# RWKV's transfers around the forward substitution: issued by GpSimd instead of SyncE

## Chip, cores and metric

One core of one Trainium2 chip. The metric is the device time of one execution of the whole program in microseconds, the median of several runs. Engines are named as in the profile: PE = TensorE, DVE = VectorE, ACT = ScalarE, POOL = GpSimd, SP = SyncE. A DMA is issued by an engine's queue; here every DMA is issued by SP.

## What is computed

One layer (1024 tokens, width 1024) of a hybrid decoder trunk. The part around the change is the RWKV-7 group: four heads of 64, a state updated token by token.

```python
def step(S, inp):
    r_t, w_t, k_t, v_t, kk_t, a_t = inp
    sa = jnp.einsum('bhvk,bhk->bhv', S, -kk_t)
    S = S * w_t[:, :, None, :] + sa[..., None] * (kk_t * a_t)[:, :, None, :] + v_t[..., None] * k_t[:, :, None, :]
    return S, jnp.einsum('bhvk,bhk->bhv', S, r_t)
...
mix = jnp.concatenate([y_conv, y_nsa, y_rwkv], axis=-1)
x = x + mix @ w_out[i]
```

Beside it stand a convolution group (31 taps, LayerNorm) and a sparse-attention group; all three go through one output projection, then a gated MLP and a final norm follow.

## The kernel before

The kernel works in the stages projections (with RWKV and convolution beside them, to about 380 us), attention (from about 400 to 733 us, with RWKV beside it), output projection, MLP up and MLP down.

RWKV is done in chunks of 64 tokens. Two pairs of heads `j` and two halves of the sequence `h` give four units, 00, 01, 10 and 11. Each has four steps: `rwkv_prep` and `rwkv_mats` (S), `rwkv_solve` (V), `rwkv_chain` (C). They are written in the order S00 .. V00 S01 .. C00 V01 .. S10 C01 V10 S11 C10 V11 C11, all at high priority. Most of their PSUM results take turns in the two banks of the tag `rw`.

In S, the chunk matrices come out of PE and DVE masks them into `GA` (L497). The inverse of their triangular part is found in blocks of 32 x 32 by forward substitution: 31 steps, each one product (L528, `sx`) and one sum (L530, `sT`) on POOL. To bring 32 small systems into one partition layout the data passes through DRAM:

- L503: four stores `dn<-GA` (two after each of the two `GA`), each 256 pieces of 128 B;
- L506: four loads `sN<-dn`, each 32 rows of 4 KB; L528 of the first step waits for them;
- after the substitution DVE transposes the result (L532, `sTT`); L534: four stores `dt<-sT`, each 512 pieces of 32 B; L535: four stores `dtt<-sTT`, each 256 pieces of 128 B;
- in V, L543: one load `DF<-dt` and L546, L547: two loads of `dtt` into `sN`, each 512 pieces of 128 B; the first matmul (L550) waits for L543, the second (L556) for the other two.

That is 19 DMAs for a unit and 76 in all. An engine executes its list in order; a DMA that waits for data holds up what is listed behind it on the same engine. The order of each engine's list is made at build time by a scheduler with a timing model, by readiness and priority. POOL also runs the taps of the second half of the convolution channels (L279, `cacc`, fed by ACT's L278, `ctap`), the differences of the down-projection weights (L945 to L948) and two steps of each attention tile (L849, L857, `cmp`). DVE splits every weight into two parts (L121, `wlo`), which PE needs for each projection (L229), and runs the taps of the first half of the channels (L272).

Of the kernel before, what the change touches and what calls it, by code (L numbers as in the profile page):

```python
# [19 lines left out]
class K:  # L20
# [460 lines left out]
    def rwkv_mats(self, u):  # L481
        nc = self.nc
        v, s, pe = nc.vector, nc.scalar, nc.tensor
        dn = self.dram.tile([32, 32, 32], F32, name=f"dn{u.j}{u.h}")
        u.dt = self.dram.tile([16, 32, 4, 8], F32, name=f"dt{u.j}{u.h}")
        u.dtt = self.dram.tile([32, 8, 4, 32], F32, name=f"dtt{u.j}{u.h}")
        u.GA, u.GR = [], []
        for x, G in enumerate((u.GA, u.GR)):
            pts = [self.bank(u.tp) for _ in range(2)]
            for c in range(8):  # L490
                for hp in range(2):
                    r = slice(hp * 64, hp * 64 + 64)
                    pe.matmul(pts[hp][:, c * 64:c * 64 + 64], u.BK[c // 4][r, c % 4].rearrange("p a t -> p (a t)"),  # L493
                              u.r[r, c, :] if x else u.VAc[c // 4][r, c % 4, 1, :], start=True, stop=True)
            for hp in range(2):
                Gm = self.rb([P, 8, 64], name="GR" if x else "GA")
                v.tensor_tensor(Gm, pts[hp].rearrange("p (a b) -> p a b", b=64),  # L497
                                self.gmask[:, x * 64:x * 64 + 64].unsqueeze(1).to_broadcast([P, 8, 64]), op=ALU.mult)
                G.append(Gm)
                if not x:  # L500
                    for blk in range(2):
                        p0 = blk * 16 + hp * 8
                        nc.sync.dma_start(dn[p0:p0 + 8].rearrange("p s t -> s p t"), Gm[64 + blk * 32:96 + blk * 32, :, blk * 32:blk * 32 + 32])  # L503
        N = self.sN.rearrange("p (a b) -> p a b", b=32)
        for g in range(4):
            nc.sync.dma_start(N[g * 32:g * 32 + 32], dn)  # L506
        u.VA, u.KB = [], []
        for q in range(2):
            VA = self.rb([P, 4, P], name="VA")
            KB = self.rb([P, 4, P], name="KB")  # L510
            BK = u.BK[q].rearrange("p c a t -> p c (a t)")
            v.tensor_tensor(BK, BK, u.PC[:, q * 4:q * 4 + 4].unsqueeze(2).to_broadcast([P, 4, P]), op=ALU.mult)
            for dst in (VA, KB):
                pt = self.bank(u.tp)
                for c in range(4):
                    x = u.VAc[q][:, c].rearrange("p a t -> p (a t)") if dst is VA else BK[:, c, :]
                    pe.transpose(pt[:, c * P:c * P + P], x, self.idn)
                s.activation(dst.rearrange("p c x -> p (c x)"), pt, AF.Copy)
            u.VA.append(VA)
            u.KB.append(KB)  # L520

        Tm = self.sT
        nc.gpsimd.tensor_copy(Tm, self.sI)
        for q in range(31):
            n, w = 31 - q, q // 4 + 1
            x = self.sx[:, 0:n * w].rearrange("p (a b) -> p a b", b=w)
            v_ = getattr(nc, self.B["sub"])
            v_.tensor_tensor(x, N[:, q, q + 1:32].unsqueeze(2).to_broadcast([P, n, w]),  # L528
                            Tm[:, q, 0:w].unsqueeze(1).to_broadcast([P, n, w]), op=ALU.mult)
            v_.tensor_tensor(Tm[:, q + 1:32, 0:w], Tm[:, q + 1:32, 0:w], x, op=ALU.add)  # L530
        sTT = self.sTT.rearrange("p a b -> p (a b)").rearrange("p (a b) -> p a b", b=32)
        v.tensor_copy(sTT, Tm.rearrange("p a b -> p b a"))  # L532
        for g in range(4):
            nc.sync.dma_start(u.dt[:, :, g, :], Tm[g * 32:g * 32 + 16])  # L534
            nc.sync.dma_start(u.dtt[:, :, g, :], sTT[g * 32:g * 32 + 32])  # L535

    def rwkv_solve(self, u):
        nc = self.nc
        s, pe = nc.scalar, nc.tensor

        TT = self.sN.rearrange("p (a b) -> p a b", b=64)
        DF = self.DF
        nc.sync.dma_start(DF[64:96], u.dt.rearrange("p s g c -> s p (g c)"))  # L543
        nc.gpsimd.memset(TT[96:128, :, 0:32], 0.0)
        dtt = u.dtt.rearrange("p c g t -> (c g) p t")
        nc.sync.dma_start(TT[64:96, :, 0:32], dtt[:, 0:16])  # L546
        nc.sync.dma_start(TT[96:128, :, 32:64], dtt[:, 16:32])  # L547
        pt = self.bank("rw")
        for p in range(16):
            pe.matmul(pt[96:128, p * 32:p * 32 + 32], u.GA[p // 8][64:96, p % 8, 32:64], DF[64:96, p, :], start=True, stop=True,  # L550
                      tile_position=(64, 96))

        s.activation(DF[96:128].rearrange("p a (c g) -> p a c g", g=4), pt[96:128].rearrange("p (a g c) -> p a c g", g=4, c=8), AF.Copy)
        pt = self.bank("rw")
        for p in range(16):
            pe.matmul(pt[64:96, p * 32:p * 32 + 32], DF[96:128, p, :], TT[96:128, p, 32:64], start=True, stop=True,  # L556
                      tile_position=(96, 64))
        s.activation(TT[64:96, :, 32:64], pt[64:96].rearrange("p (a b) -> p a b", b=32), AF.Copy)

        pa = self.bank("rw")  # L560
        for c in range(8):
            for hp in range(2):
                pe.matmul(pa[hp * 64:hp * 64 + 64, c * 64:c * 64 + 64], u.VA[c // 4][64:128, c % 4, hp * 64:hp * 64 + 64],
                          TT[64:128, hp * 8 + c, :], start=True, stop=True)
        s.activation(u.AT.rearrange("p a b -> p (a b)"), pa, AF.Copy)
        for hp in range(2):
            x = slice(hp * 64, hp * 64 + 64)
            W = self.rt(name="W")
            pt = self.bank("rw")
            for c in range(8):  # L570
                pe.matmul(pt[64:128, c * 64:c * 64 + 64], u.GA[hp][0:64, c, :], u.VA[c // 4][0:64, c % 4, x], start=True, stop=True)
            s.activation(W[64:128], pt[64:128], AF.Copy)
            pt = self.bank("rw")
            for c in range(8):
                pe.matmul(pt[64:128, c * 64:c * 64 + 64], TT[64:128, hp * 8 + c, :], W[64:128, c * 64:c * 64 + 64], start=True, stop=True)
            for q in range(2):
                s.activation(u.VA[q][64:128, :, x], pt[64:128, q * 256:q * 256 + 256].rearrange("p (c x) -> p c x", x=64), AF.Copy)
# [823 lines left out]
```

## Time and profile before

| | |
|---|---|
| median of 3 runs | 1515.36 us (1514.93 to 1518.39) |
| the profiled execution | 1516.71 us, its span 1515.0 us |
| PE busy | 1418.2 us (94% of the span) |
| DVE busy | 1001.0 us (66%) |
| ACT busy | 684.0 us (45%) |
| POOL busy | 500.2 us (33%) |
| DMA packets issued | 206564, all on SP's queue |

PE is busy nearly throughout, so a change shows in the end only where it makes or removes a time in which PE has nothing to do. A row of the timeline reads: start in us, duration, engine, line, operation, output<-inputs, shape, count; in brackets the idle time before it and what ended that.

### The profile page before, as it was taken

To read this page: it belongs to the slowest core of one execution; us is meant where nothing else is said; L and a number is where in the kernel's file an instruction comes from. 1 tells how busy PE (TensorE), PEld (TensorE's weight loads), DVE (VectorE), ACT (ScalarE), POOL (GpSimd) and SP (SyncE) were. 2 spreads that over 40 slices of the span, in tenths; PEclk is the share of its full clock that TensorE was granted. 3 is DMA by queue.
4 is the path that set the end of the run, shared out by engine and by line. 5 is a ranking of instruction groups with operands and counts; after the bars stand their busy time and mean duration, and the time that the engine had idled before them with its cause. 6 is when DMAs were issued, how large, how long until landed. Compare 5 with 4: busy or idle time off the path is not lost.

```text
span 1515.0 us, 22973 instructions
## 1 busy us (share of the span) xinstructions
PE 1418.2 (94%) x8025; PEld 1128.7 (75%) x8025; DVE 1001.0 (66%) x2171; ACT 684.0 (45%) x1361; POOL 500.2 (33%) x607
## 2 busy tenths in 40 slices
PE   6999688999798999999599899999999999999997
PEld 5887566777666777767478677888888788888886
DVE  5346696454488587777446776775876876666675
ACT  5432255534155665776333353333333443445463
POOL 1003887910487204100000133453453443113310
PEclk9999887999699999999899999999999999999999
DMA  6133223434888301310742113332332333986633
GB/s 184 36 105 80 46 77 95 146 89 119 246 259 270 101 21 41 81 43 16 226 121 84 57 56 98 105 112 84 104 119 91 104 104 111 383 295 213 207 91 111
DMA packets 206680, 186.71 MB, mean 123 GB/s; under 512 B 56355, under 2 KB 145764, under 8 KB 206564
## 3 DMA queue, kind: packets, MB, share of 16 engines
q1 hardware_dynamic: 206564, 185.24, 39.5%
q8 instruction: 63, 1.03, 0.3%
q14 instruction: 53, 0.43, 0.1%
HBM read 126.99 MB, written 58.20 MB: 122 GB/s over the span
## 4 chain that ended last, share of the span: by engine, by line
PE 78%; DVE 10%; DMA 4%; POOL 2%; issue 2%; ACT 2%; SPq 1%; DVEq 0%; ACTq 0%; POOLq 0%
PE mm L229 13%; PE gb L229 12%; PE rw L229 10%; PE ga L229 8%; PE gc L229 8%; PE tr L229 5%; PE tr L918 4%; PE av L926 4%; PE mm L893 2%; PE mm L894 2%; POOL sx L528 1%; PE rw L493 1%; POOL sT L530 1%; DVE pp L897 1%; DVE pp L911 1%
## 5 line engine op out<-in xcount | busy, mean ns | idle before, releaser
L229 PE MATMUL mm<-hT,whi 128*128 128x512 f32 x608 | 201.6, 413 | 0.0
L229 PE MATMUL mm<-hT,wlo 128*128 128x512 f32 x304 | 126.1, 416 | 18.8 <-DVE wlo L121 18.8
L229 PEld LDWEIGHTS mm<-hT,whi 128*128 128x128 f32 x608 | 118.3, 197 | 28.5 <-issue 1.4
L921 ACT ACTIVATE pT<-tr 128x512 f32<-128x512 f32 (+1 forms) x152 | 79.8, 536 | 62.1 <-PE tr L918 59.0
L926 PE MATMUL av<-pT,V 128*64 128x128 f32 x1056 | 96.4, 289 | 1.3 <-ACT pT L921 1.1
L279 POOL TENSOR_TENSOR cacc<-cacc,ctap 128x512 f32<-128x512 f32 x60 | 91.6, 1550 | 15.0 <-ACT ctap L278 14.9
L229 PE MATMUL rw<-woh,mix 128*128 128x512 f32 x240 | 79.4, 406 | 17.0 <-ACT mix L120 17.0
L918 PE MATMUL tr<-idn,pp 128*128 128x128 f32 x528 | 91.6, 292 | 0.5 <-DVE pp L911 0.3
L121 DVE TENSOR_TENSOR sp<-rb,sp 128x512 fp32r<-128x512 f32 x66 | 57.1, 865 | 50.4 <-ACT sp L120 50.3
L1072 POOL TENSOR_TENSOR S<-wraw,wr 128x512 f32<-128x512 f32 x22 | 28.5, 1295 | 181.0 <-DVE or L107 79.2
L229 PEld LDWEIGHTS mm<-hT,wlo 128*128 128x128 f32 x304 | 59.9, 197 | 37.0 <-DVE wlo L121 20.1
L893 PE MATMUL mm<-KH,QS 128*128 128x512 f32 (+2 forms) x192 | 77.3, 407 | 10.0 <-DVE mx L897 7.7
L229 PE MATMUL rw<-sp,sp 128*128 128x512 f32 x330 | 86.1, 389 | 0.0
L229 PE MATMUL tr<-sp,sp 128*128 128x512 f32 x330 | 85.9, 389 | 0.0
L926 PEld LDWEIGHTS av<-pT,V 128*64 128x64 f32 x1056 | 59.9, 138 | 27.3 <-issue 13.0
L528 POOL TENSOR_TENSOR sx<-sN,sT 128x60 f32<-128x60 f32 (+24 forms) x124 | 47.4, 382 | 97.4 <-DMA sN<-dn 90.5
L918 PEld LDWEIGHTS tr<-idn,pp 128*128 128x128 f32 x528 | 56.5, 142 | 30.0 <-issue 27.9
L120 ACT ACTIVATE sp<-rb 128x512 fp32r<-128x512 f32 x66 | 41.6, 630 | 74.0 <-PE tr L229 37.5
L121 DVE TENSOR_TENSOR sp<-b,sp 128x512 fp32r<-128x512 f32 x88 | 68.8, 789 | 5.3 <-ACT sp L120 5.1
L229 PEld LDWEIGHTS rw<-sp,sp 128*128 128x128 f32 x330 | 62.0, 188 | 12.8
L229 PEld LDWEIGHTS tr<-sp,sp 128*128 128x128 f32 x330 | 62.0, 188 | 12.8
L904 ACT ACTIVATE pp<-pp,nm 128x640 f32<-128x640 f32 (+3 forms) x64 | 57.6, 904 | 23.7 <-DVE nm L902 22.1
(457 smaller groups left out, 3721.0 us busy)
## 6 DMA issues: line engine op xcount, KB each, us to landing
wraw<-in_ffn_w_up_dram SPq DMA_DIRECT2D x44, 256.0 KB
wr<-in_ffn_w_gate_dram SPq DMA_DIRECT2D x44, 256.0 KB
pdS<-prod SPq DMA_DIRECT2D x44, 256.0 KB
b<-pdS SPq DMA_DIRECT2D x44, 256.0 KB
rb<-tdT SPq DMA_DIRECT2D x44, 256.0 KB
pdA<-prod SPq DMA_DIRECT2D x33, 256.0 KB
b<-pdA SPq DMA_DIRECT2D x33, 256.0 KB
wraw<-in_w_in_dram SPq DMA_DIRECT2D x30, 256.0 KB
```

The source lines that it names most:

```text
L120: self.nc.scalar.activation(hi, src, AF.Copy)
L121: getattr(self.nc, eng).tensor_tensor(lo, src, hi.bitcast(F32), op=ALU.subtract)
L229: mm = lambda l, r, **k: self.nc.tensor.matmul(out, l, r, skip_group_check=more, **k)
L279: nc.gpsimd.tensor_tensor(t[:, o:o + 512], t[:, o:o + 512], z, op=ALU.add)
L528: v_.tensor_tensor(x, N[:, q, q + 1:32].unsqueeze(2).to_broadcast([P, n, w]), Tm[:, q, 0:w].unsqueeze(1).to_broadcast([P, n, w]), op=ALU.mult)
L893: pe.matmul(pts[g][:, 0:n], QS[:, r, g, :], KH[g][hf][:, ks], start=True, stop=False)
L894: pe.matmul(pts[g][:, 0:n], QS[:, r, g, :], KL[g][hf][:, ks], start=False, stop=True)
L904: s.activation(Ps[g], Ps[g], AF.Exp, bias=nm[:, g:g + 1], scale=-1.0, accum_out=sm[:, g:g + 1])
L918: pe.transpose(pt[:, o:o + P], Ps[g][:, kt * P:kt * P + P], self.idn)
L921: s.activation(pT[:, 0:n], pt[:, 0:n], AF.Copy)
L926: pe.matmul(av[g * 64:g * 64 + 64, r * P:r * P + P], self.V[kk // 2][:, kk % 2, vo + g * 64:vo + g * 64 + 64], pT[:, o:o + P], start=first ...
L1072: gp.tensor_tensor(t, x, y, op=op)
```

## The change

All 76 of these DMAs are issued by GpSimd's queue instead of SP's. Nothing else is edited: sizes, layouts, buffers and the order in which the program is written stay. The lists of all engines are made anew by the scheduler.

```diff
@@ rwkv_mats
-                        nc.sync.dma_start(dn[p0:p0 + 8].rearrange("p s t -> s p t"), Gm[64 + blk * 32:96 + blk * 32, :, blk * 32:blk * 32 + 32])
+                        nc.gpsimd.dma_start(dn[p0:p0 + 8].rearrange("p s t -> s p t"), Gm[64 + blk * 32:96 + blk * 32, :, blk * 32:blk * 32 + 32])
         for g in range(4):
-            nc.sync.dma_start(N[g * 32:g * 32 + 32], dn)
+            nc.gpsimd.dma_start(N[g * 32:g * 32 + 32], dn)
...
         for g in range(4):
-            nc.sync.dma_start(u.dt[:, :, g, :], Tm[g * 32:g * 32 + 16])
-            nc.sync.dma_start(u.dtt[:, :, g, :], sTT[g * 32:g * 32 + 32])
+            nc.gpsimd.dma_start(u.dt[:, :, g, :], Tm[g * 32:g * 32 + 16])
+            nc.gpsimd.dma_start(u.dtt[:, :, g, :], sTT[g * 32:g * 32 + 32])
@@ rwkv_solve
-        nc.sync.dma_start(DF[64:96], u.dt.rearrange("p s g c -> s p (g c)"))
+        nc.gpsimd.dma_start(DF[64:96], u.dt.rearrange("p s g c -> s p (g c)"))
         nc.gpsimd.memset(TT[96:128, :, 0:32], 0.0)
         dtt = u.dtt.rearrange("p c g t -> (c g) p t")
-        nc.sync.dma_start(TT[64:96, :, 0:32], dtt[:, 0:16])
-        nc.sync.dma_start(TT[96:128, :, 32:64], dtt[:, 16:32])
+        nc.gpsimd.dma_start(TT[64:96, :, 0:32], dtt[:, 0:16])
+        nc.gpsimd.dma_start(TT[96:128, :, 32:64], dtt[:, 16:32])
```

## Rows read from the trace of the kernel before

**Rows 1.** Windows: span, busy us of each engine, PE clock, DMA share, GB/s

```profile
150.00:180.00 30.00, 17.99 (x79) 13.33 (x78) 16.44 (x23) 5.08 (x9) 22.27 (x52) 0.83 0.10 17
560.00:640.00 80.00, 79.86 (x701) 61.60 (x699) 61.98 (x242) 48.08 (x122) 21.20 (x66) 1.00 0.23 56
...
sum 1515.00, PE 1418.16 PEld 1128.75 DVE 1001.02 ACT 683.98 POOL 500.18; mean PE 88.63 PEld 70.55 DVE 62.56 ACT 42.75 POOL 31.26
```

**Rows 2.** Instructions of tiles dn, dt, dtt: ns of one issue, min/median/max

```profile
L503 SPq DMA_DIRECT2D dn<-GA x16: 302/442/568, 125.0 to 579.1; - x16
L506 SPq DMA_DIRECT2D sN<-dn x16: 302/414/647, 132.1 to 582.4; - x16
...
L534 SPq DMA_DIRECT2D dt<-sT x16: 561/608/1107, 173.5 to 617.1; - x16
...
L535 SPq DMA_DIRECT2D dtt<-sTT x16: 549/613/1012, 178.2 to 617.7; - x16
```

**Rows 3.** Timeline of unit 00, DVE, SP, POOL and PE, 129 to 180 us

```profile
129.17 0.69 DVE L497 TENSOR_TENSOR GA<-pm,gmask 128x512 f32<-128x512 f32 x1 [2.40 <-PE pm L493]
...
132.12 1.71 SPq L506 DMA_DIRECT2D sN<-dn  x4
...
136.26 0.39 POOL L528 TENSOR_TENSOR sx<-sN,sT 128x31 f32<-128x31 f32 x1 [37.59 <-DMA sN<-dn]
...
160.27 0.34 POOL L530 TENSOR_TENSOR sT<-sT,sx 128x76 f32<-128x76 f32 x1
...
173.51 0.69 DVE L532 COPY sTT<-sT 128x256 f32<-128x256 f32 x1 [13.49 <-POOL sT L530]
...
174.85 0.79 PE L229 MATMUL mm<-hT,wlo 128*128 128x512 f32 x1 [11.60 <-DVE wlo L121]
...
179.73 1.19 PE L550 MATMUL rw<-DF,GA 32*32 32x32 f32 x32 [0.42 <-DMA DF<-dt]
```

**Rows 4.** Waits of 182 to 260 us: total us, times, longest

```profile
ACT ctap L278 <- POOL cacc L279: 25.1, 28, 4.8
...
PE mm L229 <- DVE wlo L121: 7.2, 2, 4.0
```

**Rows 5.** Timeline of unit 10 ahead of its substitution, 392 to 407 us

```profile
392.70 0.69 DVE L497 TENSOR_TENSOR GA<-rw,gmask 128x512 f32<-128x512 f32 x1 [1.93 <-PE rw L493]
...
396.29 1.06 SPq L503 DMA_DIRECT2D dn<-GA  x2
...
400.37 1.72 SPq L506 DMA_DIRECT2D sN<-dn  x4
...
404.67 0.24 POOL L528 TENSOR_TENSOR sx<-sN,sT 128x31 f32<-128x31 f32 x1 [16.36 <-DMA sN<-dn]
...
406.05 0.36 PE L893 MATMUL mm<-KH,QS 128*128 128x256 f32 x1 [2.24 <-DMA QS<-qd]
```

**Rows 6.** Timeline of unit 10 behind its substitution, 503 to 516 us

```profile
503.11 0.46 POOL L530 TENSOR_TENSOR sT<-sT,sx 128x8 f32<-128x8 f32 x1
...
509.65 0.62 SPq L535 DMA_DIRECT2D dtt<-sTT  x1
511.35 0.33 SPq L543 DMA_DIRECT2D DF<-dt  x1
...
514.90 1.19 PE L550 MATMUL rw<-DF,GA 32*32 32x32 f32 x32
```

**Rows 7.** Timeline of PE (unit 11 begins) and SP (RWKV's last store, first load behind)

```profile
531.66 1.12 PE L415 MATMUL rw<-lora,lw_w 32*128 32x512 f32 x2
...
736.02 0.43 SPq L638 DMA_DIRECT2D md<-gz  x1
...
741.14 0.43 SPq L984 DMA_DIRECT2D mix<-md  x1
```

**Rows 8.** Timeline of POOL, two single instructions

```profile
380.53 2.47 POOL L669 COPY kcmp<-kcmp 128x128 f32<-128x128 f32 x1 [44.45 <-PE mm L229]
...
407.26 1.29 POOL L945 TENSOR_TENSOR wraw<-whi,wraw 128x512 f32<-128x512 f32 x1 [0.39 <-DVE mx L897]
```

## The prediction

> **What bounds the kernel now.** I read the windows first: PE is busy 1418.2 of 1515.0 us, so 96.8 us in all can be lost or won on it; 12.0 of them lie in 150 to 180 us, while 560 to 640 us has next to none [rows 1]. Next the instructions of the tiles that the 76 DMAs touch: how long SP is held by one issue [rows 2]. Then the timeline around each of the four substitutions, on all engines, for what waits for the handovers [rows 3, 5, 6]; last the end of the attention, to see whether RWKV or the attention sets it [rows 7].
>
> Two things are to be seen. In unit 00 SP stands at L534 until the substitution ends at 173.5, but so does DVE at L532 (13.49 us idle), and PE's stall of 11.60 us waits for a weight split behind that DVE copy, not for a load behind SP [rows 3]. Freeing SP does not end that stall: POOL's substitution does, and it stays. And from unit 10 on RWKV is one serial path: the `rw` banks are handed out in the written order, so S11 (L415 at 531.66) begins as V10 ends, then C10, V11 and C11 follow. C11's store of `gz` at 736.02 comes 5.1 us ahead of the first load of `mix` for the output projection at 741.14 [rows 7]. A store takes 1.1 to 3.0 us from the end of its issue to the issue of the load that reads it (510.27 to 511.35, and 397.35 to 400.37) [rows 5, 6]. So RWKV's slack there is 741.14 - 736.45 - (1.1 to 3.0) = 1.7 to 3.6 us; I take the middle, 2.7.
>
> **The change part by part.** What is removed: SP's issues, 0.41 to 0.61 us each at the median [rows 2]. With 19 DMAs a unit that is some 10 us of SP, and its waits with them. SP's list matters at one place, 392 to 406 us, where it is full of key loads: two `dn`, the wait for them and four `sN` stand there from 396.29 to 402.09, and PE then waits 2.24 us for `QS` [rows 5]. Gone from SP, this wait falls: up to -2.2 us. What is late next is the serial RWKV path, so I count 0 in the sum and keep -2.2 for the range.
>
> What is added: the same issues on POOL, in its one list with the substitution itself. No row shows a DMA issued by POOL, so I bound the issue, c. Below: SP's 0.4 to 0.6 us [rows 2]. Above: POOL's longest single row that I use, 2.47 us. I take c = 1.3 us, the 128x512 instruction of POOL at 1.29 us [rows 8], because a transfer of 256 to 512 pieces is nearer to a long instruction of POOL's programmable cores than to an issue of SP.
>
> Unit 10, ahead of the substitution. `GA` is ready at 393.39. Now the last two `dn` start 396.29, are issued by 397.35, `sN` starts 400.37 (3.0 later), is issued by 402.09, and the first step runs at 404.67 (2.6 later) [rows 5]. POOL has been idle for 16.36 us there, so it can start at once: 393.4 + 2c + 3.0 + 4c + 2.6 = 406.8 with c = 1.3, 2.1 us late.
>
> Unit 10, behind it. The substitution ends at 503.57; SP had issued the eight stores by 510.27, `DF` 1.08 later, and PE began L550 3.55 after that issue began [rows 6]. On POOL: 503.6 + 8c + 1.1 + (c - 0.33) + 3.55 = 519.6, 4.7 us late. While POOL waits for `dt` to land, `cmp` steps and weight differences queue behind it; by 503 us the differences are over.
>
> Both together make V10 6.8 us late. S11, C10, V11 and C11 move with it; less the slack of 2.7 that is **+4.1 us** at the output projection. Units 01 and 11 wait for their turn in the `rw` banks rather than for these transfers; I count them at nothing; were that cover gone, each would cost up to the same 6.8.
>
> Unit 00, ahead. `GA` is ready at 129.86, `sN` starts 2.26 later, of which some 0.9 is two issues, and the first step runs 2.4 after the four issues end [rows 2, 3]. On POOL: 129.9 + 2c + 1.4 + 4c + 2.4 = 141.5, 5.2 us late. But 13 of the 31 steps run to 160.61 at 1.87 us a step, beside DVE's work, and the other 18 in 12.9 us, at 0.72, once DVE waits [rows 3]. A late start moves 5.2 / 1.87 = 2.8 steps into the quick stretch: the end is 2.8 x 0.72 = 2.0 us late, and with it `sTT` and PE's stall: **+2.0 us**.
>
> The Trainium skill, page "SBUF — State Buffer", section on SBUF's two separate sides, speaks against the change: transfers issued by GpSimd have their descriptors written by its cores, which are locked out while DVE runs certain modes. The 1.87 against 0.72 us above is a lock of this sort between POOL's and DVE's arithmetic; no row shows it for descriptors.
>
> Unit 00, behind. The eight stores and `DF` hold POOL some 12 us from 175.5, so L550 could start 16.0 us after the substitution (unit 10's sum), at 191.5 instead of 179.73. PE waits 0.42 us there now [rows 3]. With PE's list as it is, that would be a stall of 11.8 us; a list made anew can put L550 later, which costs nothing. On the other side POOL's taps start later, and DVE and ACT, between which PE waits 7.2 us for `wlo` in 182 to 260 us, are freer of them; yet ACT's splits stand in one list with `ctap`, which already waits 25.1 us for POOL's taps [rows 4], and gives the relief back. The ends are -7.2 and +11.8; I take 0, since the row nearest to it is the 0.42 us that the scheduler's order left here.
>
> **Sum:** +4.1 + 2.0 = +6.1 us. The profiled execution took 1516.7 us (span 1515.0 and 1.7 around it): 1522.8. It is 1.3 above the median, 1515.4, against which the runs will stand: **1521.5 us**.
>
> **The rivals.** *Faster.* If POOL issues almost as quickly as SP, c up to 0.8, the same sums give unit 10 -0.9 ahead and +0.2 behind: within the slack. Then the `QS` wait counts (-2.2), and the pause of the taps lets DVE run ahead (-7.2), with unit 00 about 1 late: 1515.4 - 2.2 - 7.2 + 1 = 1507. For it: the 7.2 us are true DVE waits, and POOL has two thirds of its span idle. Against: 12 fewer microseconds of taps now are 12 more later. It decides below c = 0.8.
>
> *No change.* The terms exist but are hidden or cancel: c near 0.8 to 1.0, V10 inside its slack, L550 placed later: 1512 to 1519. The Trainium skill, page "DMA: Bandwidth & Descriptors", section on issuing engines not being separate queues, says that another issuing engine only saves the sequencer's issue time; by that rule the forecast is this case.
>
> *Clearly slower.* POOL is held per piece, c = 2.5. Unit 10: 393.4 + 5 + 3.0 + 10 + 2.6 = 414.0, 9.3 late; behind it 503.6 + 20 + 1.1 + 2.2 + 3.55 = 530.4, 15.5 late; less 2.7: +22.1. Unit 00: 12.4 late at the start, 6.6 steps, +4.7. In all +26.8: 1542. For it: an issue of 512 pieces takes SP 0.61 us, one of 32 rows 0.41 [rows 2], so pieces cost even there. Against: 19 issues of 2.5 us, 48 us a unit, would be longer than unit 00's whole substitution.
>
> **How the numbers follow.** Forecast (1520 to 1530) 0.30; faster (1500 to 1511) 0.28; no change 0.24; clearly slower (1530 to 1555) 0.18. 0.3%, 4.5 us, is about what a measurement of this kernel can tell from no change. Faster 0.28, within 0.24, slower 0.48. The range takes in c from 0.4 to 2.5 and leaves out about a tenth at each side: 1504 to 1543. The forecast's own range is 1520 to 1530.
>
> **What would show it.** POOL's rows of the 76 issues give c directly: 1.3 expected, under 0.8 the faster case, 2.5 the slow one. The first L528 of unit 00 should come near 141 instead of 136, PE's stall should still wait for `wlo` behind `sTT`. The interval from the last L530 of unit 10 to L550 should be 16 instead of 11.3 us, and `gz`'s last store should come some 7 us later against the first `mix` load. The prediction is wrong if the engines' new lists differ more than these intervals: if the taps of POOL, or the `cmp` steps behind waiting DMAs, become what PE waits for, or if the units 01 and 11 have no cover.

## The result and the profile after

The changed kernel took 1541.05 us (median of 4 runs, 1539.61 to 1548.77) beside 1516.88 us (4 runs, 1514.93 to 1523.27) of the kernel before: ratio 1.0167, 95% interval 1.0137 to 1.0196, 24 us slower. The forecast was 1521.5. Its sign was right and its whole range of 1504 to 1543 holds the time; the forecast's own range, 1520 to 1530, does not.

The profiled execution of the changed kernel took 1548.77 us (span 1547.1), the longest of the four, so some 8 of the 32.1 us by which the span grew belong to this execution and not to the median. Its busy times, and its whole span in four stages (the columns are those of [rows 1]): to the first matmul of the attention (L839), to its last (L926), to the first load of `mix`, and the rest. Behind them stand the same stages of the kernel before:

```profile
PE 1439.7 (93%) x8025; PEld 1143.8 (74%) x8025; DVE 1006.3 (65%) x2171; ACT 683.5 (44%) x1361; POOL 538.4 (35%) x683
```

```profile
0.00:418.76 418.76, 369.93 (x1948) 297.73 (x1948) 218.76 (x434) 161.10 (x313) 180.85 (x284) 0.88 0.36 103
418.76:757.51 338.75, 325.22 (x2805) 239.90 (x2804) 259.42 (x892) 207.73 (x478) 130.34 (x221) 0.96 0.35 105
757.51:773.01 15.50, 1.71 (x7) 0.71 (x6) 4.84 (x8) 3.15 (x5) 0.00 (x0) 0.67 0.89 286
773.01:1547.10 774.09, 742.86 (x3268) 605.51 (x3268) 523.28 (x838) 311.55 (x565) 227.18 (x178) 0.99 0.41 134
```

```profile
0.00:400.06 400.06, 354.63 (x1947) 285.05 (x1948) 226.06 (x436) 161.47 (x313) 162.85 (x242) 0.91 0.38 105
400.06:732.01 331.95, 318.20 (x2805) 236.76 (x2806) 249.31 (x891) 207.87 (x478) 109.17 (x187) 0.97 0.37 111
732.01:741.14 9.13, 1.64 (x6) 0.64 (x6) 3.34 (x5) 2.42 (x4) 0.00 (x0) 0.81 0.70 207
741.14:1515.00 773.86, 743.69 (x3268) 606.29 (x3268) 522.32 (x839) 312.21 (x566) 228.16 (x178) 0.99 0.42 137
```

The first stage is 18.7 us longer, the second 6.8, the third 6.4, and the last 0.2. Over the whole span PE idles 107.4 instead of 96.8 us (+10.6) and is busy 21.5 us longer with the same 8025 matmuls. The second part goes with the clock: its mean grant over the span is 0.947 instead of 0.962, and 1418.2 us times 0.962/0.947 is 1441, an estimate near the measured 1439.7. Most of it lies in the first stage (15.3 us more busy, 3.4 more idle). There PE idles 5.9 us up to 222.2; from 226.9 to 261.0 us the granted clock is 0.50, which is 1.2 instead of 2.4 GHz. In the kernel before PE idles 4.9 us up to 229.1, and the 0.50 lasts from 232.6 to 246.2. Why it lasts longer in the changed kernel was not tested.

The instructions of the moved tiles (count; ns min/median/max, first and last start), as in [rows 2]:

```profile
L503 POOL DMA_DIRECT2D dn<-GA x16: 582/582/784, 123.6 to 602.2; - x16
L506 POOL DMA_DIRECT2D sN<-dn x16: 489/502/817, 131.5 to 606.2; - x16
...
L534 POOL DMA_DIRECT2D dt<-sT x16: 640/651/668, 173.9 to 643.9; - x16
...
L535 POOL DMA_DIRECT2D dtt<-sTT x16: 558/600/651, 178.4 to 647.1; - x16
```

An issue on POOL takes 0.50 to 0.65 us at the median (0.69 with `DF`, L543), against the 1.3 that the prediction took, and little more than SP's of the same groups. By the prediction's own rivals that is the *faster* case, and yet the time is that of the slow one. So the cost is somewhere else. A timeline of unit 00 behind its substitution (the answer to [rows 3]):

```profile
173.41 0.70 DVE L532 COPY sTT<-sT 128x256 f32<-128x256 f32 x1 [14.06 <-POOL sT L530]
174.76 0.80 PE L229 MATMUL mm<-hT,wlo 128*128 128x512 f32 x1 [9.29 <-DVE wlo L121]
178.44 2.32 POOL L535 DMA_DIRECT2D dtt<-sTT  x4
183.15 0.72 POOL L543 DMA_DIRECT2D DF<-dt  x1
202.29 1.19 PE L550 MATMUL rw<-DF,GA 32*32 32x32 f32 x32
```

The substitution ends where it did, PE's stall still waits for `wlo` behind `sTT`, and `DF` is issued at 183.15, 5.4 us later than before. But L550 runs at 202.29 instead of 179.73, with no wait in front of it: it simply stands 74 matmuls later in PE's list, at the 798th instead of the 724th of the list as built (the trace counts 842 and 768). POOL's list changed too. Timeline of POOL at unit 01:

```profile
237.00 1.16 POOL L503 DMA_DIRECT2D dn<-GA  x2 [4.86 <-DVE GA L497]
...
245.95 1.02 POOL L506 DMA_DIRECT2D sN<-dn  x2
255.55 0.97 POOL L506 DMA_DIRECT2D sN<-dn  x2 [8.58 <-PE rw L575]
258.23 2.51 POOL L279 TENSOR_TENSOR cacc<-cacc,ctap 128x512 f32<-128x512 f32 x2 [1.71 <-ACT ctap L278]
260.71 0.23 POOL L528 TENSOR_TENSOR sx<-sN,sT 128x31 f32<-128x31 f32 x1
```

Two of unit 01's four `sN` loads wait until V00's last matmul (L575) has read that tile, which V00 fills with `dtt`, and POOL waits 8.58 us with them. Of POOL's 61 operations on the convolution's sum (one L274, then the 60 taps L279; called taps below) only 27 stand ahead of substitution 01 (38 before), the other 34 among its steps (23 before), so it lasts from 260.7 to 336.9 (255.1 to 311.4 before), and the last tap ends at 326.2 instead of 295.8. The taps' group and the loads' in the view that groups POOL's lines, 180 to 330 us (busy, mean ns | idle before them), and the taps' group of the kernel before:

```profile
L279 POOL TENSOR_TENSOR cacc<-cacc,ctap 128x512 f32<-128x512 f32 x60 | 87.9, 1479 | 24.0 <-ACT ctap L278 23.7
...
L506 POOL DMA_DIRECT2D sN<-dn x4 | 2.0, 502 | 8.6 <-PE rw L575 8.6
```

```profile
L279 POOL TENSOR_TENSOR cacc<-cacc,ctap 128x512 f32<-128x512 f32 x60 | 91.6, 1550 | 15.0 <-ACT ctap L278 14.9
```

The attention starts 18.7 us later (L839 at 418.8, before 400.1), its last matmul ends 25.5 us later (757.5, before 732.0), and the first load of `mix` for the output projection starts 31.9 us later (the answer to [rows 7]):

```profile
762.76 1.22 SPq L638 DMA_DIRECT2D md<-gz  x1
...
773.01 0.38 SPq L984 DMA_DIRECT2D mix<-md  x1
```

The last store of `gz` now stands 10.3 us ahead of that load, not 5.1. SP's list was made anew as well: between the two it issues 12 other DMAs (weights, `xn` and the norm's row) where it issued 7. That the serial RWKV path carries the delay is not shown: RWKV and the attention end together, before and after, and about 5 us are added behind both. The kernels below that have the changed kernel's list on PE (x2, z2) show nearly the same, 9.9 and 10.0 us.

### The profile page after: what moved, and what is told of

It reads as the page before. It is cut to its first block, busy times and chain, and to the rows that moved or that the text cites. A ratio compares the mean times of both kernels' runs of the same rounds, so it can differ in the third digit from the quotient of the medians.

```text
span 1547.1 us, 23020 instructions
## 1 busy us (share of the span) xinstructions
PE 1439.7 (93%) x8025; PEld 1143.8 (74%) x8025; DVE 1006.3 (65%) x2171; ACT 683.5 (44%) x1361; POOL 538.4 (35%) x683
## 4 chain that ended last, share of the span: by engine, by line
PE 78%; DVE 9%; DMA 4%; POOL 3%; issue 3%; ACT 2%; SPq 1%; DVEq 0%; ACTq 0%; POOLq 0%
PE mm L229 12%; PE gb L229 12%; PE rw L229 10%; PE ga L229 8%; PE gc L229 8%; PE tr L229 5%; PE av L926 4%; PE tr L918 4%; PE mm L893 2%; PE mm L894 2%; PE pm L493 1%; DVE pp L911 1%; POOL sT L530 1%; DVE pp L897 1%; POOL sx L528 1%
## 5 line engine op out<-in xcount | busy, mean ns | idle before, releaser
L926 PE MATMUL av<-pT,V 128*64 128x128 f32 x1056 | 96.7, 291 | 0.9 <-ACT pT L921 0.9
L279 POOL TENSOR_TENSOR cacc<-cacc,ctap 128x512 f32<-128x512 f32 x60 | 87.9, 1479 | 24.0 <-ACT ctap L278 23.7
L893 PE MATMUL mm<-KH,QS 128*128 128x512 f32 (+2 forms) x192 | 76.2, 403 | 10.6 <-DVE mx L897 10.6
L926 PEld LDWEIGHTS av<-pT,V 128*64 128x64 f32 x1056 | 59.8, 139 | 27.2 <-issue 14.4
L229 PEld LDWEIGHTS rw<-woh,mix 128*128 128x128 f32 x240 | 46.3, 194 | 33.9 <-ACT mix L120 24.2
L120 ACT ACTIVATE whi<-wraw 128x512 fp32r<-128x512 f32 x55 | 34.4, 628 | 79.0 <-PE mm L229 58.3
## 6 DMA issues: line engine op xcount, KB each, us to landing
wr<-in_ffn_w_gate_dram SPq DMA_DIRECT2D x44, 256.0 KB
wraw<-in_ffn_w_up_dram SPq DMA_DIRECT2D x44, 256.0 KB
pdS<-prod SPq DMA_DIRECT2D x44, 256.0 KB
b<-pdS SPq DMA_DIRECT2D x44, 256.0 KB
rb<-tdT SPq DMA_DIRECT2D x44, 256.0 KB
pdA<-prod SPq DMA_DIRECT2D x33, 256.0 KB
b<-pdA SPq DMA_DIRECT2D x33, 256.0 KB
wraw<-in_w_in_dram SPq DMA_DIRECT2D x30, 256.0 KB
```

Source lines behind the costliest of these rows:

```text
L120: self.nc.scalar.activation(hi, src, AF.Copy)
L229: mm = lambda l, r, **k: self.nc.tensor.matmul(out, l, r, skip_group_check=more, **k)
L279: nc.gpsimd.tensor_tensor(t[:, o:o + 512], t[:, o:o + 512], z, op=ALU.add)
L893: pe.matmul(pts[g][:, 0:n], QS[:, r, g, :], KH[g][hf][:, ks], start=True, stop=False)
L926: pe.matmul(av[g * 64:g * 64 + 64, r * P:r * P + P], self.V[kk // 2][:, kk % 2, vo + g * 64:vo + g * 64 + 64], pT[:, o:o + P], start=first ...
```

## The experiments

Two theories stood after this: **lists** (the order that the scheduler made anew costs, whatever issues the transfers) and **issue and wait on POOL** (the DMAs and their waits in POOL's in-order list cost, whatever the order). To hold a list, the kernel of the wanted order is built first, its instructions are read off per engine, and the kernel to run is built with every one of them, the DMAs that are moved excepted, tied behind its predecessor. The tie orders issue and adds no wait for data. The lines in the source of the runs y1 to z2:

```diff
+            for e, names in like.items():
+                names = [n for n in names if n in by and str(by[n].engine).split(".")[-1] == e]
+                for p, n in zip(names, names[1:]):
+                    tc.add_manual_dep(by[n], p, info, reason="list")
...
+    made = {"before": lists_of(build(inputs, ((),) * 3)[0])}
```

All of them in one table: PE's first matmul of V00, substitution 01, the end of the last tap and the attention's first L839 in us of each profiled execution; then the median less that of the kernel before in the same comparison, and the ratio with its interval.

| kernel | V00 | substitution 01 | last tap | L839 | median | ratio (95%) |
|---|---|---|---|---|---|---|
| before | 179.7 | 255.1–311.4 | 295.8 | 400.1 | | |
| changed | 202.3 | 260.7–336.9 | 326.2 | 418.8 | +24.2 | 1.0137–1.0196 |
| x1: changed, all lists of before | 182.9 | 262.6–322.4 | 306.8 | 408.7 | +11.7 | 1.004–1.011 |
| x2: before, all lists of changed | 197.1 | 256.0–331.9 | 321.2 | 413.5 | +15.6 | 1.007–1.015 |
| x3: changed, PE's list of before | 188.2 | 280.1–339.9 | 321.9 | 428.3 | +25.8 | 1.0089–1.0218 |
| x4: changed, POOL's list of before | 187.8 | 272.6–328.9 | 312.4 | 393.6 | +12.1 | 1.0059–1.012 |
| y1: before's lists, unit 01 ahead moved | 178.4 | 257.2–312.8 | 297.9 | 400.0 | +5.6 | 1.0002–1.006 |
| y2: before's lists, unit 10 ahead moved | 178.3 | 253.1–309.3 | 293.6 | 397.4 | +3.9 | 0.9999–1.0051 |
| y3: before's lists, all behind moved | 179.4 | 252.6–308.7 | 293.0 | 395.3 | -0.2 | 0.9971–1.0027 |
| p23: all behind moved, lists free | 186.1 | 242.3–312.9 | 300.5 | 399.9 | +0.7 | 0.9994–1.0037 |
| z1: before, POOL's list of changed | 177.8 | 247.3–323.8 | 313.9 | 407.6 | +14.0 | 1.0059–1.0109 |
| z2: before, PE's list of changed | 204.5 | 262.4–318.0 | 301.5 | 419.5 | +30.7 | 1.0187–1.0238 |
| w1: before, taps behind substitution 01 | 177.3 | 252.2–309.4 | 350.8 | 432.9 | +28.6 | 1.0175–1.0244 |
| w2: before, taps ahead of substitution 01 | 178.8 | 292.4–318.5 | 292.5 | 400.4 | -5.8 | 0.9949–0.999 |

**x1, x2: lists or transfers.** x1 has the changed DMAs and the old lists, x2 the old DMAs and the changed lists.

> The changed kernel with one thing fixed: every engine's list (PE, DVE, ACT, POOL, SP, but for the 76 moved DMAs) is held in the order that it has in the kernel before; only the places of the 76 DMAs in POOL's list are free. Theory 'lists': the loss comes from the lists that were made anew (V00's first matmul of unit 00 stands 74 matmuls later in PE's list, the taps stand among the steps of substitution 01), not from the issue or the landing of the transfers. Then only the handovers of after remain: unit 00's first matmul of V00 would wait some 6 us for its DF load (last step to DF landed, 173.4 to about 186, against PE's arrival at 179.7), unit 10's 6 us longer handover less 2.7 of slack would cost 3: 1517 to 1527 us. Theory 'issue and wait on POOL': the DMAs and their waits in POOL's list cost the time, whatever the lists: 1535 to 1549 us, as the changed kernel.

> The kernel before, its 76 DMAs on SP, with every engine's list (but for the 76 DMAs) held in the order that it has in the changed kernel. Theory 'lists': most of the loss is here without a single DMA on POOL, 1530 to 1545 us. Theory 'issue and wait on POOL': with the DMAs back on SP the time is that of before, 1512 to 1522 us, since nothing stands in POOL's list that waits for a load.

1530.55 and 1534.44 us, beside 1518.89 of the kernel before. Neither theory alone: the lists cost 15.6 us with not one DMA on POOL, the transfers cost 11.7 with not one other instruction moved. Together that is 27, against the 24 of the whole change; that the two add up is not shown, since the transfers meet another order of instructions in each. x1 misses both of its ranges; x2 lies in that of 'lists'. The two lose in different ways. x1's PE is busy 1417.9 us, as before (1418.2), and idles 14.7 us longer, so there an idle microsecond costs itself and no more. x2's PE idles 5.4 us longer and is busy 15.7 us longer, with a mean granted clock of 0.952 (0.952 to 0.956 in its four executions, 0.956 to 0.965 in x1's six). The longer busy time of the changed kernel thus comes with its lists. Where x1's transfers cost is seen first in POOL's timeline at unit 01:

```profile
255.91 1.98 POOL L506 DMA_DIRECT2D sN<-dn  x4
257.91 4.72 POOL L279 TENSOR_TENSOR cacc<-cacc,ctap 128x512 f32<-128x512 f32 x3
262.61 0.23 POOL L528 TENSOR_TENSOR sx<-sN,sT 128x31 f32<-128x31 f32 x1
```

The issues stand among the taps: POOL does two taps between the last `dn` and the `sN`, and three between the `sN` and the first step. That step comes at 262.6 instead of 255.1, the last tap 11 us later.

**y1, y2, y3: which transfers.** All lists are those of before; only part of the 76 is moved. One line differs between the three runs; it names the units whose `dn` and `sN`, whose `dt` and `dtt`, and whose loads in V (`DF` and `dtt`) GpSimd issues (y1, y2, y3):

```diff
+GP = (('01',), (), ())
...
+GP = (('10',), (), ())
...
+GP = ((), ('00', '01', '10', '11'), ('00', '01', '10', '11'))
```

> All lists as in the kernel before; only the four stores of dn and the four loads of sN of unit 01 are issued by GpSimd. Theory 'place behind the taps': these issues stand among the taps in POOL's list, so they leave only when POOL has done the taps ahead of them; substitution 01 starts some 7 us later (255.1 before, 262.6 with all transfers moved) and ends some 11 later, and the projections and the attention follow it: 6 to 11 us over the kernel before. Rival 'slow transfers': it is only that a transfer by GpSimd's queue takes longer to land; without the taps' part the start would be 2 to 3 us late: 0 to 4 us over the kernel before.

> All lists as in the kernel before; only the four stores of dn and the four loads of sN of unit 10 are issued by GpSimd. Theory 'SP set free': the loads of keys, queries and down weights that stood behind these issues and their wait on SP now leave at once, fill the 16 DMA engines and sN lands 6 to 9 us after its issue instead of 2.6 after the last; POOL waits for it with the attention's L849 behind, and PE stands 5 to 9 us at L893: 4 to 9 us over the kernel before. Rival 'slack' (the prediction's view): substitution 10 is 2 to 4 us late, SP's relief takes the 2.24 us wait for QS away, and the sum is -2 to +3 us.

> All lists as in the kernel before; dn and sN stay on SP, the transfers behind the substitutions (dt, dtt, DF and the two loads of dtt) of all four units are issued by GpSimd. Theory 'ahead of the substitutions': the cost lies in dn and sN, and these 44 transfers cost next to nothing: the interval from the last step to L550 in unit 10 stays 11.3 us, unit 00 waits some 2 us at L550: 0 to 4 us over the kernel before. Theory 'issue time' (the prediction's own term, at the measured 0.5 to 0.7 us an issue): unit 10's interval grows by 8 x 0.65 - 6.6, so nothing, and unit 00's L550 is held 3 us: the same 0 to 4. Rival 'waits in POOL's list': 8 or more over, since the taps stand behind DMAs that wait for sTT and dt to land.

Medians of 1522.29, 1520.6 and 1516.57 us, beside 1516.73. The 44 transfers behind the substitutions cost nothing that can be measured (-0.2 us, interval -4.4 to +4.1). In unit 10 of y3 the interval from the last step to L550 is 8.4 us (11.3 before), and PE waits 0.50:

```profile
499.36 0.20 POOL L530 TENSOR_TENSOR sT<-sT,sx 128x8 f32<-128x8 f32 x1
...
507.94 1.19 PE L550 MATMUL rw<-DF,GA 32*32 32x32 f32 x32 [0.50 <-DMA DF<-dt]
```

y2 shows how 8 DMAs of one unit can cost. Its profiled execution is its longest (1526.07 us), that of y1 its shortest (1516.74), so the rows show a mechanism and not the size of the median. Its timeline of POOL and PE, and its DMA row for 396 to 412 us in 40 slices (tenths of 16 engines) with the loads' median from issue to landing (last number); then the DMA row of the kernel before for the same stretch:

```profile
398.09 1.99 POOL L506 DMA_DIRECT2D sN<-dn  x4 [5.30 <-DMA dn<-GA]
406.58 0.24 POOL L528 TENSOR_TENSOR sx<-sN,sT 128x31 f32<-128x31 f32 x1 [6.50 <-DMA sN<-dn]
414.30 0.80 PE L893 MATMUL mm<-KH,QS 128*128 128x512 f32 x1 [9.44 <-DVE mx L897]
```

```profile
DMA  9999999999999999999999964100000000000892
...
sN<-dn POOLq DMA_DIRECT2D x4, 128.0 KB, 6.4
```

```profile
DMA  6999769978510698892499977989999999998899
```

With SP no longer held at `sN`, the key, query and weight loads behind it leave at once: the 16 engines are full without a gap until 405 us, and `sN` lands 6.4 us after its issue (x1: 7.8; over all sixteen in the changed kernel the median is 3.3). POOL waits for it in order, the attention's L849 stands behind that wait, and PE stands 9.44 us at L893. The changed kernel itself does not show this wait: at its unit 10 the row is as full (share 1.00 at 422.6 to 428.9 us), yet `sN` lands 4.4 us after its issue, POOL, which has weight differences between, waits 0.84 us, and PE waits 2.5 us at most at L893 (9.2 in x1). So a full row alone does not give the 6.4 us, and what x1 and y2 lose at this place is not part of the 24 us. The 2.24 us wait for `QS` of [rows 5] is gone, as the prediction said; this wait took its place. y2's interval touches 1, so its 3.9 us, between its two ranges, is not secured; the mechanism is in the rows. In y1 the first step is 2.1 us late, not 7, and the measured 5.6 us has a wide interval (0.3 to 9 us): between theory and rival. Counted from the end of DVE's `GA` (L497) the step is 3.4 us late in y1 and 4.1 in x1; the other 3.4 of x1's 7.5 us are there when `GA` comes (251.99, before 248.62), behind a V00 that is 3.2 us late.

**z1, z2, x3, x4: which list.** One engine's list is held, the others are the scheduler's for that.

> The 76 transfers on SP as in the kernel before; only POOL's list (but for the DMAs) is held as in the changed kernel: 27 taps ahead of substitution 01 (38 before) and 34 among its steps (22 before). V00 of unit 00 stands at PE's 724th matmul, as before; the other lists are the scheduler's. Theory 'taps among the steps': substitution 01 takes some 75 us instead of 56, and the time is 10 to 18 us over the kernel before. Theory 'place of V00 on PE': it stands as before, so 0 to 5 us over.

> The 76 transfers on SP; only PE's list is held as in the changed kernel: V00 of unit 00 at the 798th matmul (724 before); the other lists are the scheduler's, with 38 taps ahead of substitution 01, as before. Theory 'taps among the steps' (POOL's list): substitution 01 takes some 56 us as before, and the time is 0 to 6 us over the kernel before. Theory 'place of V00 on PE': V00 comes 15 to 20 us late, S01's loads of sN wait for its last matmul, and the time is 10 to 18 us over.

> The changed kernel with PE's list alone held as in the kernel before (V00 of unit 00 at its 724th matmul again); the lists of DVE, ACT, POOL and SP are made by the scheduler for that. In it 40 of POOL's 60 taps stand ahead of substitution 01 (27 in the changed kernel, 38 before). Theory 'place of V00 on PE': that place alone carries the loss, so this is within 5 us of the kernel with all lists of before, 1515 to 1530 us. Theory 'taps among the steps on POOL': the two go together here, and the same is expected. Theory 'issue and wait on POOL': 1535 to 1549 us.

> The changed kernel with only POOL's list (but for the DMAs) held as in the kernel before, so that 38 taps stand ahead of substitution 01 again; the other lists are the scheduler's. V00 of unit 00 stands at PE's 772nd matmul (724 before, 798 changed). Theory 'place of V00 on PE': still late by 48 matmuls of 0.22 to 0.4 us, some 12 to 18 us: 1530 to 1545 us. Theory 'taps among the steps on POOL': with the taps out of the way substitution 01 takes its 56 us again and the loss goes: 1515 to 1527 us.

Either list alone is enough to lose: z1 1530.76 and z2 1547.40 us, beside 1516.73 and 1516.71. z1 lies in the range of 'taps among the steps'. In it POOL reaches substitution 01 with 27 taps done, waits 17.40 us for `sN`, and 34 taps wait behind it:

```profile
247.31 0.33 POOL L528 TENSOR_TENSOR sx<-sN,sT 128x31 f32<-128x31 f32 x1 [17.40 <-DMA sN<-dn]
...
323.58 0.20 POOL L530 TENSOR_TENSOR sT<-sT,sx 128x8 f32<-128x8 f32 x1
```

In z2 POOL is nearly in time (last tap 301.5), but PE's list isn't. V00 runs at 204.5, SP's second half of the `sN` loads waits for V00's end, and the convolution's sum L284, which has had its input since 301.5, runs at 332.3 (297.6 before):

```profile
204.49 1.19 PE L550 MATMUL rw<-DF,GA 32*32 32x32 f32 x32
...
259.34 0.77 SPq L506 DMA_DIRECT2D sN<-dn  x2
...
332.30 1.02 PE L284 MATMUL tr<-cacc,ones 128*128 128x512 f32 x2
```

This is twice what 'place of V00 on PE' gave. PE's list puts L284 late too, and runs it without a wait in front; which of the list's places costs how much was not separated, since the whole list was held. Given back alone, POOL's list takes the loss down to that of x1 (x4, 1530.99 us, against the theory of the taps and at the low end of 'place of V00 on PE'). PE's does not help at all (x3, 1544.68 us), against both of x3's list theories; the range of 'issue and wait on POOL' holds that time, but x1, with the same transfers, is 14 us below it. PE waits there for what the other engines' lists bring late:

```profile
188.21 1.91 PE L550 MATMUL rw<-DF,GA 32*32 32x32 f32 x32 [22.34 <-DMA DF<-dt]
...
216.08 1.19 PE L229 MATMUL mm<-hT,whi 128*128 128x512 f32 x2 [14.40 <-DVE ev L686]
```

**p23: lists free for the harmless part.**

> The transfers behind the substitutions (dt, dtt, DF and the loads of dtt) of all units by GpSimd, dn and sN on SP, and the lists made anew by the scheduler. With the lists held as before these 44 transfers cost nothing (1516.57 against 1516.73 us). In the lists made anew 30 taps stand ahead of substitution 01 (38 before, 27 in the changed kernel) and V00 of unit 00 stands at PE's 758th matmul (724 before). Theory 'lists': the lists alone cost, here between a third and all of the 12.7 us that POOL's list of the changed kernel cost: 4 to 13 us over the kernel before. Theory 'issue and wait on POOL': the same transfers as with the lists held, so 0 to 3 us over.

1517.42 us beside 1516.71: 'lists' missed. New lists, with 30 taps ahead and V00 at the 758th matmul, cost nothing that can be measured here (interval -0.9 to +5.6 us); the last tap ends at 300.5. So it is not that lists are made anew, but which: in the changed kernel the last tap ends 30 us late.

**w1, w2: the taps alone.** The kernel before, with the 22 or 23 taps that stand among the steps of substitution 01 in POOL's list moved to one side:

```diff
...
+    mid = names[a:b + 1]
+    taps = [n for n in mid if outs(n).startswith("cacc_")]
+    rest = [n for n in mid if n not in taps]
+    return names[:a] + (rest + taps) + names[b + 1:]
```

That is w1; w2 has `(taps + rest)` in the last line.

> The kernel before with one change in POOL's list: the taps that stand among the steps of substitution 01 are moved behind its last step; the other lists are the scheduler's for that. The other sign of the changed kernel's list. Theory 'substitution 01 sets the path': it takes 27 instead of 56 us and ends near 283 instead of 311.4; what it drives (V01, S10, the attention's start, the wait of 13.3 us at the output projection) comes earlier: 2 to 12 us under the kernel before. Rival 'the taps set it': the last tap ends near 312 instead of 295.8, the convolution's statistics (L284) follow it, and the gain is given back: 0 to 10 us over.

> The kernel before with one change in POOL's list: the taps that stand among the steps of substitution 01 are moved ahead of its first step, all 60 then. Theory 'POOL's work only': 22 taps of 1.28 us go ahead, the substitution starts 28 us later, takes 28 us less and ends where it did: -2 to +4 us. Rival 'ACT's products': the taps wait for ctap (7.31 us at 252 in the kernel before), so POOL stands, the substitution ends 5 to 15 us later, and the time is 4 to 12 us over.

w1 took 1545.26 us, w2 1510.87, beside 1516.71; both miss both of their ranges. w1 is no clean test of its theory: a memset of the next unit stands among the steps and waits 31.39 us for DVE, so the substitution ends 2 us earlier and not 28. But it shows that late taps go with a late kernel: the last ones come 55 us late, and L284 53 us.

```profile
303.63 0.10 POOL L360 MEMSET rraw<- 128x1 f32 x1 [31.39 <-DVE rkv L369]
...
349.53 1.28 POOL L279 TENSOR_TENSOR cacc<-cacc,ctap 128x512 f32<-128x512 f32 x1 [0.70 <-ACT ctap L278]
```

```profile
351.02 1.02 PE L284 MATMUL tr<-cacc,ones 128*128 128x512 f32 x2
```

w2 is the other end: all taps are done by 292.5, the substitution runs without them in 26 us, ends 7 us later than before, and that costs nothing: 7 us of lateness there are free as long as the taps are in time. It beats both kernels, by 0.1 to 0.5% against the one before, which is about as little as can be told apart; by which later wait it gains was not settled.

```profile
292.40 0.24 POOL L528 TENSOR_TENSOR sx<-sN,sT 128x31 f32<-128x31 f32 x1
...
318.34 0.20 POOL L530 TENSOR_TENSOR sT<-sT,sx 128x8 f32<-128x8 f32 x1
```

## Why the prediction was right, and where it was wrong

The sign came out, by another way than the sum's. That the range holds the time is luck: its upper end was there for c = 2.5, and with the c that was measured the prediction's own sums give 1507.

- **The price of an issue** (1.3 us taken): 0.50 to 0.69. Mis-sized by a factor of two, and with it the variable on which all cases were hung was the wrong one. "It decides below c = 0.8" fails: c lies there, and the time is 1541.
- **Unit 10, behind** (+4.7): nothing. With the lists held the interval stays 11.3 us (x1, 516.0 to 527.3) or falls to 8.4 (y3). The 17.4 us of the changed kernel (524.8 to 542.2) is again L550's place in PE's list: it runs there without a wait, and x2, with no DMA on POOL, has 16.8. So it is by luck that V10, counted from `GA`, is 6.4 us later in the changed kernel, near the 6.8 of the sum.
- **Unit 10, ahead** (+2.1): the direction is right, the reason is not. From the first L493 to the first step x1 takes 22.1 us instead of 18.3 (395.8 to 417.9, 386.4 to 404.7), 3.8 more. The terms that were wrong are the two landings taken over from [rows 5]: 2.6 us from the last issue to the first step is 6.5 (y2) to 8.0 us (x1), and 3.0 us from `dn` to `sN` is 5.3 in y2, where SP, set free, fills the DMA engines. In the changed kernel the step is 3.3 us late from `GA`, and the substitution's end 0.3. The prediction saw SP's list and counted only the wait that vanishes (-2.2), not what SP would issue.
- **Unit 00, ahead** (+2.0): the mechanism holds. Counted from the end of `GA`, the first step is 2.3 us late in x1 and 2.5 in the changed kernel, the end 1.1 and 1.6: part of the lateness is taken back. The 5.2 us at the start were too much, with the price of the issues.
- **The slack of 2.7**, taken off the sum: no run shows it. In the kernels with the lists of before the first `mix` load starts 5.1 to 5.3 us behind `gz`'s store (x1, y1, y2, y3), though that store comes up to 13.7 us later (x1): SP issues the same seven DMAs between. In the changed kernel the store came 5.1 us earlier against that load, not 7 later.
- **Unit 00, behind** (-7.2 to +11.8, taken 0): the step that failed. With the lists of before PE waits 2.1 (x1) to 3.1 us (y3) at L550, not 11.8 (which counts the 16.0 us from 175.5; from the substitution's end at 173.5 they give 9.8). "A list made anew can put L550 later, which costs nothing" does not hold for the lists in which it stands later here: x2 costs 15.6 us, z2 30.7. L550's place itself has no wait, but V00's end releases the tile for unit 01's `sN` (in z2 at 259.31, the loads at 259.34), and the same lists move the taps and L284. The prediction's last part named this as what would make it wrong ("the taps of POOL ... become what PE waits for"), and gave it no price.
- **Units 01 and 11, at nothing.** Unit 01 had little cover: 5.6 us in y1 (interval 0.3 to 9), more with V00 late (x1). The prediction set the turn in the `rw` banks against it, but the taps share POOL's list and feed the convolution, and in x1 the last of them ends 11 us late. Unit 11 was not run alone.
- **The Trainium skill's rules.** DVE was busy 65% of the span and no issue on POOL took over 0.82 us, nor did one land over 5.1 us after its issue in the changed kernel. The Trainium skill's page "SBUF — State Buffer" (section on SBUF's two separate sides) describes a lock that keeps GpSimd from writing descriptors. These rows show no stall that must be that lock; whether it has a part in the spread of `sN`'s landings (2.5 to 4.7 us) they cannot tell. The rule of the Trainium skill's page "DMA: Bandwidth & Descriptors" (section on issuing engines not being separate queues), by which another issuing engine saves issue time alone, agrees with y3 (ratio 0.9999), not with x1 (1.0075), where the place in an in-order list costs.

Open: why the scheduler makes these lists when `dn` and `sN` are moved too (p23 shows that the others don't bring them about) was not run; nor was a tile of its own for V00's `dtt`, which would cut the tie from V00's end to unit 01's loads. What the transfers cost under the changed lists (24.2 less 15.6 us) was not located, since x1's wait at L893 is not there. Which places in PE's list make up z2's 30.7 us, and what makes the granted clock fall for longer with the changed lists, stays open too.

## What to carry to other kernels

Where a scheduler makes the engines' lists, an edit to one queue is two changes, the edit and the new lists; hold the lists of the kernel before, or the new ones, and you can price each alone, here 11.7 and 15.6 us (they need not add up, and need not cost by the same waits as together). A DMA that is moved into a compute engine's list cost here by its place there (what stands ahead of it, what waits behind its landing), hardly by its issue. And when a queue is set free, write down what it will issue at that moment, and onto which engines that falls.

## What the hardware showed that was not expected

- POOL's median issue in the changed kernel is 0.50 us for a DMA of 32 rows, 0.58 to 0.60 for 256 pieces and 0.65 to 0.69 for 512: sixteen times the pieces add 0.15 to 0.19 us. SP's for the same DMAs were 0.34 (`DF`) to 0.61 us.
- The same 128 KB load (`sN` from `dn`) lands 3.3 us after its issue at the median, and 6.4 to 7.8 us after it in unit 10 of y2 and x1, where loads of another queue fill the 16 engines; in unit 10 of the changed kernel, with the engines as full, it is 4.4.
- The same 8025 matmuls kept PE busy 1418.2 us before and 1439.7 after, at a mean granted clock of 0.962 and 0.947. More idle time does not always bring this: x1's PE idles 14.7 us more than before, with the clock at 0.960 and 1417.9 us busy.
